# Batched 64x64 matmul on one core: b cast two tiles ahead into three bf16 buffers

## The chip, the cores and the metric

One core of one Trainium2 chip runs the kernel. The metric is the device time of one execution in microseconds (us). Before the change three runs gave 134.10, 134.24 and 134.47 us, median 134.24 us.

## The reference

`a` and `b` are float32 arrays of 1024 matrices of 64x64; the result is their product, matrix by matrix, in float32.

```python
def reference(a, b):
    return np.matmul(a, b).astype(np.float32)
```

The kernel rounds both operands to bf16 and accumulates in float32.

## The kernel before, in words

**Tiles.** The 1024 matrices are 16 tiles t of 64 matrices (`n_t` = 16), and two tiles make one step s of `a` (`n_s` = 8). A tile of b is 1 MB in float32, the result of a tile is 1 MB, a step of a is 2 MB.

**What becomes of b.** `load_b(t)` (L94 to L98) issues one DMA of a whole tile into a float32 buffer `b_sb`, of which there are three (`B_AHEAD = 3`); even tiles are issued on the queue of SyncE (SP), odd tiles on that of ScalarE (ACT). `cast(t)` (L169 to L181) turns `b_sb` into `b_bf`, a bf16 copy of which there are two buffers (pool `work`). Casts run on VectorE (DVE, L173) but for tile 0 (ACT, L173) and tile 15 (two quarters on ACT, L180, and two on DVE, L178). A load of tile t+3 may start when cast(t) has emptied its `b_sb`.

**What becomes of a.** `load_first_a` brings step 0 through SP and ACT into buffers of the result pool (L91). `load_a(s)` brings the others: three DMAs on the GpSimd (POOL) queue that cast to bf16 on the way (`a_sb`, L74), and one on SP that doesn't (`a_raw`, L78). There are three buffers of each. For the steps 0, 1, 6 and 7 `regroup` gathers the rows into `a_bf` (L106 for step 0; L109 and L112, on DVE, for the others), `transpose` turns pairs of columns on TensorE (PE, L138) and ACT copies the result to `at_sb` (L141). For the steps 2 to 5 (`ON_DVE`) `transpose_dve` does this on DVE (L128) with one cast of `a_raw` on ACT (L126). `spread(t)` then copies `at_sb` on DVE (L164, or L154 for the steps 2 to 5) into one of two block-diagonal tiles `at_bd`. It may overwrite it when the product of tile t-2 has been computed.

**The product.** `multiply(t)` issues 64 matmuls (L218) from `at_bd` and `b_bf` into two halves `o_ps` in PSUM, and eight copies (L206) from there to `o_sb`: on ACT, but for two of the eight on DVE in tiles 11 and 13, and half of them on DVE in tile 15. `store(t)` sends `o_sb` to the result one tile later (L195): on POOL up to tile 13, on SP and ACT for the last two.

**What sets the order.** The body is written out under a manual schedule: each engine runs its instructions in the order of the program text, and waits are for data and for free buffers. A DMA stands in the queue of the engine that issues it, in that engine's order. In iteration t of the main loop the order is this:

```python
if t + 1 < n_t:
    spread(t + 1)
    cast(t + 1)
if t + B_AHEAD < n_t:
    load_b(t + B_AHEAD)
...
multiply(t)
if t == 0:
    regroup(1)
    load_a(A_AHEAD)
    load_a(A_AHEAD + 1)
    transpose(1, 0)
    transpose(1, 1)
```

So on DVE cast(1) stands between spread(1) and regroup(1), and cast(2) behind spread(2). After `multiply` the other iterations have `transpose_dve`, `regroup` or `transpose` for step s+2. On SP the DMAs before the loop are those of `a` for step 0, b tile 0, `a_raw` of step 1, b tile 2 and `a_raw` of step 2; in the loop `a_raw` of steps 3 and 4 are issued in iteration 0, and b tile 4 behind them in iteration 1.

Of the kernel before, what the change touches and what calls it, by code (L numbers as in the profile page):

```python
# [9 lines left out]
bf16 = mybir.dt.bfloat16  # L10
# [3 lines left out]
def kernel(  # L14
# [19 lines left out]
    n_t, n_s = B // 64, B // 128  # L34
    A_AHEAD = 3
    B_AHEAD = 3
# [9 lines left out]
    a_pool = ctx.enter_context(tc.tile_pool(name="a_pool", bufs=A_AHEAD))  # L46
    b_pool = ctx.enter_context(tc.tile_pool(name="b_pool", bufs=B_AHEAD))
    work = ctx.enter_context(tc.tile_pool(name="work", bufs=2))
    o_pool = ctx.enter_context(tc.tile_pool(name="o_pool", bufs=8))
    t_psum = ctx.enter_context(  # L50
        tc.tile_pool(name="t_psum", bufs=4, space=bass.MemoryType.PSUM)
# [18 lines left out]
    def load_a(s):  # L70

        a_sb = a_pool.tile([128, 3, 16, 64], bf16, name="a_sb")
        for h in range(3):
            nc.gpsimd.dma_start(  # L74
                out=a_sb[:, h, :, :].rearrange("p v k -> p (v k)"), in_=a_v[s, h], single_packet=True
            )
        a_raw = a_pool.tile([128, 16, 64], fp32, name="a_raw")
        nc.sync.dma_start(out=a_raw[:].rearrange("p v k -> p (v k)"), in_=a_v[s, 3])  # L78
        a_tiles[s] = a_sb, a_raw

    def load_first_a():

        raw = [
            o_pool.tile([128, 8, 2, 2, 64], fp32, name="o_sb")[:].rearrange(
                "p gh j wl n -> p (gh j wl n)"
            )
            for _ in range(2)
        ]
        parts = [raw[h % 2][:, 1024 * (h // 2) : 1024 * (h // 2) + 1024] for h in range(4)]
        for h in range(4):  # L90
            (nc.scalar if h % 2 else nc.sync).dma_start(out=parts[h], in_=a_v[0, h])  # L91
        a_tiles[0] = parts

    def load_b(t):  # L94
        b_sb = b_pool.tile([128, 16, 128], fp32, name="b_sb")
        queue = nc.scalar if t % 2 else nc.sync
        queue.dma_start(out=b_sb[:], in_=b_v[t])  # L97
        b_tiles[t] = b_sb  # L98

    def regroup(s):  # L100
        a_sb = a_tiles.pop(s)
        a_bf = work.tile([128, 16, 4, 64], bf16, name="a_bf")
        if s == 0:
            for h in range(4):
                copy = nc.scalar.copy if h % 2 else nc.vector.tensor_copy
                copy(a_bf[:, :, h, :], a_sb[h].rearrange("p (v k) -> p v k", v=16))  # L106
        else:
            cast_sb, raw = a_sb
            nc.vector.tensor_copy(  # L109
                a_bf[:, :, 0:3, :], cast_sb[:].rearrange("p h v k -> p v h k")  # L110
            )
            nc.vector.tensor_copy(a_bf[:, :, 3, :], raw[:])  # L112
        abf_tiles[s] = a_bf
        at_tiles[s] = work.tile([128, 32, 4, 4, 4], fp32, name="at_sb")

    def transpose_dve(s, half):
        cast_sb, raw = a_tiles[s]
        if half == 0:
            at_tiles[s] = work.tile([128, 4, 8, 4, 4, 4], fp32, name="at_sb")
        for h in (2 * half, 2 * half + 1):  # L120
            rows = cast_sb[:, h, :, :] if h < 3 else None
            if h == 3:
                rows = work.tile([128, 16, 4, 64], bf16, name="a_bf")[:, 0:4, :, :].rearrange(
                    "p x y k -> p (x y) k"
                )
                nc.scalar.copy(rows, raw[:])  # L126
            pairs = rows.rearrange("p v k -> p (v k)").bitcast(fp32)
            nc.vector.transpose(  # L128
                at_tiles[s][:, h].rearrange("p g w mp vo -> p w vo g mp"),
                pairs.rearrange("p (vo w kp) -> p w vo kp", vo=4, w=4),  # L130
            )

    def transpose(s, j):
        a_cols = abf_tiles[s][:].rearrange("p v h k -> p v (h k)").bitcast(fp32)
        for wl in range(2):
            at_ps = t_psum.tile([128, 4, 128], fp32, name="at_ps")
            for vo in range(4):
                nc.tensor.transpose(  # L138
                    at_ps[:, vo, :], a_cols[:, 4 * vo + 2 * j + wl, :], identity[:]
                )  # L140
            nc.scalar.copy(  # L141
                at_tiles[s][:, :, 2 * j + wl, :, :],
                at_ps[:].rearrange("p vo (g mp) -> p g mp vo", mp=4),
            )

    def spread(t):
        bd = bd_tiles[t % N_BD]
        at_sb = at_tiles[t // 2]
        for h in range(4):
            rows = slice(32 * h, 32 * h + 32)  # L150
            if t // 2 in ON_DVE:
                for i in range(2):
                    block = 32 * (2 * (t % 2) + i)
                    nc.vector.tensor_copy(  # L154
                        bd[rows, 8 * i : 8 * i + 8, :, h, :, :].rearrange(
                            "p g w mp vo -> p (g w) (mp vo)"
                        ),
                        at_sb[block : block + 32, h].rearrange(
                            "p g w mp vo -> p (g w) (mp vo)"
                        ),  # L160
                    )
            else:
                half = slice(16 * (t % 2), 16 * (t % 2) + 16)
                nc.vector.tensor_copy(  # L164
                    bd[rows, :, :, h, :, :].rearrange("p g w mp vo -> p (g w) (mp vo)"),
                    at_sb[rows, half].rearrange("p g w mp vo -> p (g w) (mp vo)"),
                )

    def cast(t):  # L169
        b_bf = work.tile([128, 16, 128], bf16, name="b_bf")  # L170
        b_sb = b_tiles.pop(t)
        if t < n_t - 1:
            (nc.vector.tensor_copy if t else nc.scalar.copy)(b_bf[:], b_sb[:])  # L173
        else:
            for gq in range(4):
                rows = slice(4 * gq, 4 * gq + 4)
                if gq % 2:
                    nc.vector.tensor_copy(b_bf[:, rows, :], b_sb[:, rows, :])  # L178
                else:
                    nc.scalar.copy(b_bf[:, rows, :], b_sb[:, rows, :])  # L180
        bbf_tiles[t] = b_bf  # L181

    def store(t):
        for piece in held.pop(t):
            piece()
# [53 lines left out]
    with tc.manual_schedule():  # L239
        load_first_a()  # L240

        nc.vector.memset(warm[:, 0:1], 0.0)
        nc.scalar.copy(warm[:, 1:2], warm[:, 0:1])
        load_b(0)
        load_b(1)
        nc.vector.memset(bd_tiles[0][:], 0.0)  # L246
        make_identity(nc, identity)
        nc.gpsimd.memset(bd_tiles[1][:, 0:8], 0.0)
        load_a(1)
        load_b(2)  # L250
        nc.gpsimd.memset(bd_tiles[1][:, 8:16], 0.0)
        load_a(2)
        regroup(0)
        transpose(0, 0)
        transpose(0, 1)
        spread(0)
        cast(0)
        for t in range(n_t):
            s, half = t // 2, t % 2
            if t + 1 < n_t:  # L260
                spread(t + 1)
                cast(t + 1)
            if t + B_AHEAD < n_t:
                load_b(t + B_AHEAD)
            if half == 0 and 0 < s < n_s - 1 - A_AHEAD:
                load_a(s + 1 + A_AHEAD)
            if half == 0 and 0 < s < n_s - 1 and s + 1 not in ON_DVE:
                transpose(s + 1, 1)
# [7 lines that stand above are left out]
            if t and s + 2 in ON_DVE and (half or s):  # L276
                for part in [0, 1] if t == 1 else [half]:
                    transpose_dve(s + 2, part)
                if half:
                    a_tiles.pop(s + 2)  # L280
            elif half == 0 and 0 < s and s + 2 < n_s:
                regroup(s + 2)
            elif half == 1 and s + 2 < n_s:
                transpose(s + 2, 0)
            if t >= HOLD - 1:
                store(t - HOLD + 1)
        for t in range(n_t - HOLD + 1, n_t):
            store(t)
# [30 lines left out]
```

## Time and profile before

| | value |
|---|---|
| median of three runs | 134.24 us |
| the profiled execution | 134.24 us, of which the span of its instructions is 132.1 us |
| mean granted clock of TensorE | 0.693 |
| DVE busy | 100.7 us, 76% |
| ACT busy | 89.2 us, 68% |
| PE busy | 63.2 us, 48% |
| POOL busy | 32.0 us, 24% |
| read from HBM, written | 33.55 MB, 16.78 MB |
| cast of b on DVE (L173), mean of one | 1227 ns |
| four copies of `spread` on DVE (L164), mean of one | 724 ns |
| eight copies of `spread` on DVE (L154), mean of one | 436 ns |

How to read it: times in the text are microseconds from the start of the span. "2.1 us around the span" is the difference between the execution's time and its span. A timeline row gives the start, the time from the first instruction's start to the last one's end, the engine, the line, and in brackets how long the engine sat idle ahead of it and what ended that. DMA rows give the issuing queue (SPq, ACTq, POOLq) and the time from issue to landing. Digits in the row of an engine are its busy share in tenths, for each of 40 equal slices of 3.3 us.

### The profile page before, as it was taken

The page shows a single profiled execution, that of the slowest core. Times are in us where ns is not written, and L with a number is a line of the kernel's source. Part 1 is how long each engine was busy: PE and PEld are TensorE (multiplying, and loading weights), DVE is VectorE, ACT ScalarE, POOL GpSimd, SP SyncE. Part 2 cuts the span into 40 slices and gives each one's busy share as a digit, 9 for nine tenths or more (in the row PEclk, how much of TensorE's full clock was granted, in tenths as well). Part 3 has the DMA queues.
Part 4 walks back from the last instruction along what each step waited for, and adds up shares of the span by engine and source line. Part 5 has one row for each costly group of instructions (what it writes and reads, how often), then busy time and mean ns, then how long its engine had stood idle before and what let it go on. Part 6 is the DMA issues. An engine that isn't in the chain of part 4 may idle for free.

```text
span 132.1 us, 2719 instructions
## 1 busy us (share of the span) xinstructions
PE 63.2 (48%) x1088; PEld 60.5 (46%) x1088; DVE 100.7 (76%) x150; ACT 89.2 (68%) x159; POOL 32.0 (24%) x43
## 2 busy tenths in 40 slices
PE   0006406990733701909190737359709834677700
PEld 0006306980733701909190737259709734676700
DVE  5930399209999915999989998999999998598730
ACT  2225524999893790583989197929999996728970
POOL 8991000420074000702061302040203040312000
PEclk9999999999686555555555555555995995555555
DMA  3999999999999999999999999999999999999996
GB/s 83 351 336 310 309 313 277 288 301 327 326 305 385 371 308 298 395 385 396 327 282 357 402 395 347 296 326 387 399 392 394 394 392 387 398 399 396 364 324 201
DMA packets 19020, 44.99 MB, mean 341 GB/s; under 512 B 1088, under 2 KB 3136, under 8 KB 19008
## 3 DMA queue, kind: packets, MB, share of 16 engines
q0 software_dynamic: 6832, 20.19, 50.6%
q1 hardware_dynamic: 7120, 14.68, 30.8%
q10 hardware_dynamic: 5056, 9.96, 20.0%
q8 instruction: 8, 0.13, 0.4%
q14 instruction: 4, 0.03, 0.1%
HBM read 33.55 MB, written 16.78 MB: 381 GB/s over the span
## 4 chain that ended last, share of the span: by engine, by line
DMA 37%; DVE 27%; ACT 13%; PE 9%; issue 8%; ACTq 2%; SPq 1%
DMA b_sb<-in_b_dram 31%; DVE at_bd L154 11%; ACT o_sb L206 11%; DMA o_sb<-in_a_dram 6%; DVE b_bf L173 6%; PE o_ps L218 5%; DVE at_bd L164 4%; PE at_ps L138 3%; DVE at_sb L128 3%; DVE a_bf L109 1%; DVE a_bf L112 1%; ACTq L97 1%; ACT a_bf L126 1%; ACT a_bf L106 1%; ACT at_sb L141 1%
## 5 line engine op out<-in xcount | busy, mean ns | idle before, releaser
L206 ACT COPY o_sb<-o_ps 64x512 f32<-64x512 f32 x116 | 67.4, 581 | 19.2 <-PE o_ps L218 16.1
L218 PEld LDWEIGHTS <-at_bd 128*128 128x128 bf16 x1024 | 50.5, 125 | 52.9 <-DVE b_bf L173 44.7
L218 PE MATMUL o_ps<-b_bf,at_bd 128*128 128x64 bf16 x960 | 49.1, 231 | 49.4 <-DVE b_bf L173 42.7
L164 DVE COPY at_bd<-at_sb 32x1024 f32<-32x1024 f32 x32 | 23.2, 724 | 12.7 <-ACT at_sb L141 11.9
L154 DVE COPY at_bd<-at_sb 32x512 f32<-32x512 f32 x64 | 27.9, 436 | 1.3
L195 POOL DMA_DIRECT2D out_dram<-o_sb x14 | 15.5, 1108 | 47.5 <-ACT o_sb L206 30.7
L74 POOL DMA_DIRECT2D a_sb<-in_a_dram x21 | 12.4, 606 | 39.8 <-DVE at_sb L128 26.4
L173 DVE CAST b_bf<-b_sb 128x2048 bf16<-128x2048 f32 x14 | 17.2, 1227 | 6.4 <-DMA b_sb<-in_b_dram 6.0
L138 PE MATMUL at_ps<-identity,a_bf 128*128 128x128 f32 x64 | 11.2, 349 | 11.2 <-ACT a_bf L106 11.2
L138 PEld LDWEIGHTS at_ps<-identity,a_bf 128*128 128x128 f32 x64 | 10.3, 188 | 11.1 <-issue 11.1
L128 DVE STREAM_TRANSPOSE at_sb<-a_sb 128x512 f32<-128x512 f32 x12 | 12.0, 1062 | 0.0
L141 ACT COPY at_sb<-at_ps 128x512 f32<-128x512 f32 x16 | 8.5, 594 | 2.1 <-PE at_ps L138 2.0
L106 ACT CAST a_bf<-o_sb 128x1024 bf16<-128x1024 f32 x2 | 2.1, 1044 | 5.2 <-DMA o_sb<-in_a_dram 5.2
L128 DVE STREAM_TRANSPOSE at_sb<-a_bf 128x512 f32<-128x512 f32 x4 | 4.2, 1053 | 0.7 <-ACT a_bf L126 0.7
L126 ACT CAST a_bf<-a_raw 128x1024 bf16<-128x1024 f32 x4 | 4.2, 1046 | 0.7 <-DMA a_raw<-in_a_dram 0.6
L173 ACT CAST b_bf<-b_sb 128x2048 bf16<-128x2048 f32 x1 | 1.9, 1898 | 3.7 <-DMA b_sb<-in_b_dram 3.7
L206 DVE COPY o_sb<-at_ps 64x256 f32<-64x256 f32 x8 | 3.4, 422 | 1.3 <-PE at_ps L218 1.2
L246 DVE MEMSET at_bd<- 128x4096 f32 x1 | 3.5, 3472 | 0.8 <-issue 0.8
L218 PE MATMUL at_ps<-b_bf,at_bd 128*128 128x64 bf16 x64 | 3.6, 242 | 1.0 <-DVE at_bd L164 1.0
L106 DVE CAST a_bf<-o_sb 128x1024 bf16<-128x1024 f32 x2 | 2.8, 1385 | 1.7 <-DMA o_sb<-in_a_dram 1.7
L206 ACT COPY o_sb<-at_ps 64x256 f32<-64x256 f32 x8 | 2.9, 367 | 0.1
L180 ACT CAST b_bf<-b_sb 128x512 bf16<-128x512 f32 x2 | 1.1, 616 | 2.8 <-DMA b_sb<-in_b_dram 2.8
(16 smaller groups left out, 15.4 us busy)
## 6 DMA issues: line engine op xcount, KB each, us to landing
out_dram<-o_sb POOLq DMA_DIRECT2D x14, 1024.0 KB, 21.1
a_sb<-in_a_dram POOLq DMA_DIRECT2D x21, 256.0 KB, 16.0
a_raw<-in_a_dram SPq DMA_DIRECT2D x7, 512.0 KB, 16.9
o_sb<-in_a_dram SPq DMA_DIRECT2D x2, 512.0 KB, 5.8
o_sb<-in_a_dram ACTq DMA_DIRECT2D x2, 512.0 KB, 7.1
out_dram<-o_sb SPq DMA_DIRECT2D x2, 512.0 KB, 3.6
out_dram<-o_sb SPq DMA_DIRECT2D x2, 256.0 KB, 3.6
out_dram<-o_sb ACTq DMA_DIRECT2D x2, 256.0 KB, 3.1
```

Of the source, the lines that this page charges most:

```text
L74: nc.gpsimd.dma_start(out=a_sb[:, h, :, :].rearrange("p v k -> p (v k)"), in_=a_v[s, h], single_packet=True)
L106: copy(a_bf[:, :, h, :], a_sb[h].rearrange("p (v k) -> p v k", v=16))
L126: nc.scalar.copy(rows, raw[:])
L128: nc.vector.transpose(at_tiles[s][:, h].rearrange("p g w mp vo -> p w vo g mp"), pairs.rearrange("p (vo w kp) -> p w vo kp", vo=4, w=4),)
L138: nc.tensor.transpose(at_ps[:, vo, :], a_cols[:, 4 * vo + 2 * j + wl, :], identity[:])
L141: nc.scalar.copy(at_tiles[s][:, :, 2 * j + wl, :, :], at_ps[:].rearrange("p vo (g mp) -> p g mp vo", mp=4),)
L154: nc.vector.tensor_copy(bd[rows, 8 * i : 8 * i + 8, :, h, :, :].rearrange("p g w mp vo -> p (g w) (mp vo)"), at_sb[block : block + 32, h]. ...
L164: nc.vector.tensor_copy(bd[rows, :, :, h, :, :].rearrange("p g w mp vo -> p (g w) (mp vo)"), at_sb[rows, half].rearrange("p g w mp vo -> p ...
L173: (nc.vector.tensor_copy if t else nc.scalar.copy)(b_bf[:], b_sb[:])
L195: store_queue(t, lo).dma_start(out=o_v[t, :, lo : lo + n, :], in_=o_sb[:, lo : lo + n].rearrange("p gh j wl n -> p (gh j wl n)"),)
L206: copies[2 * par + wl](dst, src)
L218: nc.tensor.matmul(o_ps[:, gl, g % 2, j, :], at_bd[:, j, g, :, u], b_bf[:, g, 64 * u : 64 * u + 64], start=(u == 0), stop=(u == 1),)
```

## The change

`b_bf` moves out of the pool `work` (two buffers) into a pool of its own with three. Before the loop `cast(1)` is added behind `cast(0)`, with `load_b(3)` between them. In iteration t the cast is that of tile t+2 in place of t+1, and the load that of tile t+4 in place of t+3. Nothing else changes; the number of casts and loads is the same.

```diff
+    bf_pool = ctx.enter_context(tc.tile_pool(name="bf_pool", bufs=3))
...
     def cast(t):
-        b_bf = work.tile([128, 16, 128], bf16, name="b_bf")
+        b_bf = bf_pool.tile([128, 16, 128], bf16, name="b_bf")
...
         spread(0)
         cast(0)
+        load_b(B_AHEAD)
+        cast(1)
         for t in range(n_t):
             s, half = t // 2, t % 2
             if t + 1 < n_t:
                 spread(t + 1)
-                cast(t + 1)
-            if t + B_AHEAD < n_t:
-                load_b(t + B_AHEAD)
+            if t + 2 < n_t:
+                cast(t + 2)
+            if t + B_AHEAD + 1 < n_t:
+                load_b(t + B_AHEAD + 1)
```

In the changed order DVE runs spread(0), cast(1), spread(1), cast(2), regroup(1), spread(2), cast(3) and so on; SP issues b tile 4 between `a_raw` of step 2 and `a_raw` of step 3; ACT issues b tile 5 behind the copies L141 of step 1; and ACT's two quarters of cast(15) stand ahead of its copies of tile 13's result.

## The prediction

> **What bounds the kernel now.** The profiled execution took 134.24 us: its span of 132.1 us and 2.1 us around it. The median is the same 134.24 us, so sums on the span carry over. Read first the busy digits of VectorE and the DMA engines.
>
> ```profile
> DVE  5930399209999915999989998999999998598730
> DMA  3999999999999999999999999999999999999996
> ```
>
> DMA engines are busy from the second slice to the last but one. DVE is thin in slices 3 to 9 and again in 14, then full from 16 to 33. In the table by stretches DVE works 45.66 us of the 48 us from 61 to 109, and the rest is the 0.03 us between its 76 instructions; so a delay that DVE carries into this stretch isn't made up in it. The list of waits says what DVE and ACT lacked elsewhere.
>
> ```profile
> DVE at_bd L164 <- ACT at_sb L141: 11.9, 2, 6.0
> DVE b_bf L173 <- DMA b_sb<-in_b_dram: 6.0, 3, 4.2
> ACT b_bf L180 <- DMA b_sb<-in_b_dram: 2.8, 1, 2.8
> ```
>
> The columns are us in total, times, longest. The 11.9 us are startup (spread(0) and spread(2) wait for transposed a). The 6.0 are casts waiting for b: 4.2 at tile 4, then 0.41 and 1.37 at tiles 13 and 14. The 2.8 are tile 15 on ACT, and from there the chain of waits runs to the end. The change moves all of these. DVE's timeline of the startup:
>
> ```profile
> 17.61 3.50 DVE L164 COPY at_bd<-at_sb 32x1024 f32<-32x1024 f32 x5
> 21.15 1.23 DVE L173 CAST b_bf<-b_sb 128x2048 bf16<-128x2048 f32 x1
> 22.29 0.95 DVE L109 COPY a_bf<-a_sb 128x3072 bf16<-128x3072 bf16 x1
> 23.16 0.69 DVE L112 CAST a_bf<-a_raw 128x1024 bf16<-128x1024 f32 x1
> 29.84 2.83 DVE L164 COPY at_bd<-at_sb 32x1024 f32<-32x1024 f32 x4 [6.00 <-ACT at_sb L141]
> 32.71 1.23 DVE L173 CAST b_bf<-b_sb 128x2048 bf16<-128x2048 f32 x1
> ```
>
> Cast(1) comes at 21.15, regroup(1) ends at 23.85, its transposes and their copies bring spread(2) to 29.84, and cast(2) follows at 32.71. The deciding number is when b tile 2 lands. A window of the DMA view around its issue at 9.89 has only that load of b:
>
> ```profile
> b_sb<-in_b_dram SPq DMA_DIRECT2D x1, 0.5 KB, 21.8
> ```
>
> So it lands at 31.65, 1.1 us ahead of its cast in the old order. In the new order cast(2) stands ahead of regroup(1), whose data are there at 22.
>
> **Part 1, the start (loss).** spread(0) ends at 18.3. Cast(1) is next and waits for b tile 1: issued at 2.76, 17.4 us to landing, so 20.1; with 1.23 it ends at 21.4. spread(1) took 2.8 (18.33 to 21.12) and ends at 24.2. Multiply(0) isn't touched, it waits for ACT's cast(0) until 21.0. Then cast(2) waits from 24.2 to 31.65 and ends at 32.9. Behind it on DVE stand regroup(1) and all else; behind regroup(1) stand PE's 16 transposes, ahead of multiply(1) in PE's order, ACT's four copies with the issue of b tile 5, on POOL the loads of a for step 4 and store(0), on SP `a_raw` of step 4. Regroup(1) took 1.5 us from the cast's end (22.38 to 23.85): 34.4. The transposes took 3.2 (24.48 to 27.66), the last copy 0.6: 38.2. So spread(2) starts at 38.2 in place of 29.84, 8.4 late, with one cast more behind it (1.2): DVE is 7.2 us behind in work. DMA engines lose little: at 24 the tiles 2, 3 and 4 of b and some a are in the queues.
>
> **Part 2, tile 4 (gain).** The old SP order put b tile 4 behind two `a_raw` loads, the second of which waited for regroup(1).
>
> ```profile
> 51.18 1.23 DVE L173 CAST b_bf<-b_sb 128x2048 bf16<-128x2048 f32 x1 [4.24 <-DMA b_sb<-in_b_dram]
> 52.32 1.07 DVE L128 STREAM_TRANSPOSE at_sb<-a_sb 128x512 f32<-128x512 f32 x1
> ```
>
> This row also shows how a waiting cast holds DVE: the transpose behind it reads an `a_sb` of step 3, issued by 11.31 and landed, by the DMA rows, at most 21.7 us later, and still starts after the cast. In the new order tile 4 is issued at about 22, when cast(1) has freed its buffer and SP's stalled `a_raw` is out (10.64 plus 11.44). Even at the slowest landing of any b load (26.3 us) it is there at 48.4. Cast(4) comes at 38.2 plus spread(2) 2.8, cast(3) 1.2, four transposes 4.0 and spread(3) 3.0, so 49.2. The 4.2 us vanish: 7.2 - 4.2 = 3.0 us behind. Next could be tile 5: its issue on ACT moves from 35.18 to 38.2, behind the copies; at the median of 16.4 us it lands at 54.6, and cast(5) wants it at 49.2 + 1.2 + 1.9 (two transposes) + 3.4 (spread(4)) = 55.7. A margin of 1.1 us; I take no wait.
>
> **Part 3, the full stretch.** Work is the same. Two waits of DVE for ACT's cast of `a_raw` (0.40 and 0.35) go, as a cast now stands ahead of those transposes: 2.2 us behind at the end of it. The eight copies of L154 took 3.43 to 3.99 us a tile, 1.7 us over the minimum in the sum of eight tiles; the long ones lie beside POOL's issues, whose places shift: between -1 and +1, taken as 0. The third `b_bf` buffer adds no wait: cast(t+2) overwrites what multiply(t-1) read, and spread(t+1), just ahead, waits for that product already.
>
> **Part 4, the end.** Issues of b follow the casts. Cast(11) would end at 97.3 (before 99.04), so tile 14 lands at 97.3 + 16.1 = 113.4, wanted at 112.7 after spread(13): a wait of 0.7 for 1.37; tile 13's 0.41 goes. That saves 1.1. Ahead of spread(15) DVE now also has its half of cast(15), 0.8. So spread(15), which ended at 121.1, is 3.0 - 0.75 - 1.1 + 0.8 = 2.0 us late, and multiply(15) with it. On ACT the order turns against itself: cast(15) now stands ahead of tile 13's copies. Tile 15, issued about 102.5, lands at 116.9 to 118.9 (14.4 to 16.4 us), while tile 13's products are ready at about 115. Behind it ACT has 1.1 (cast), 3.6, 4.7 and 3.4 us of copies: 129.7 to 131.7, where it ended at 128.65. So this path is 1.1 to 3.1 late, DVE's 2.0. I take 1.9: **134.24 + 1.9 = 136.1 us**, with 135.2 to 137.4 for this case.
>
> The Trainium skill speaks for the change here: "DMA: Bandwidth & Descriptors", section "Anatomy of one DMA — SWDGE (gpsimd) path", fits a DMA at 2.0 us plus its bytes over 436e3 per us. That is 4.4 us for 1 MB (an estimate from that page, whose fit is for the other queue kind); tile 2 would be there at 14.3, cast(2) would wait for nothing, and 7.2 us of part 1 would fall away. The 21.8 us of this trace are five times that, so the fit isn't used.
>
> **Rivals.**
> *Faster: tile 2 lands in time.* The price of part 1 goes down by 1 us for each us that tile 2 lands earlier, down to 24.2. In the new order less of a is asked for while tile 2 is on its way, and the first loads of b landed in 16.6 and 17.4 us. Break even is at 31.65 - 1.9 = 29.7, a landing of 19.8 us; at 24.2 the wait is gone, and what is left is the gain of parts 2 to 4, limited by the DMA engines: their share is 0.87 in the 12.1 us from 120 on against some 1.06 before, (1.06 - 0.87) / 1.06 x 12.1 = 2.2 us that could be closed, so 132.0 us. Against it: all that competes with tile 2 was issued by 11.3, ahead of any change, and SP's queue ahead of it is the same.
> *Slower still: no payback.* Tile 5 takes as long as tile 2 did (21.8 in place of 16.4): cast(5) waits 4.3 us, 140.4. Half of that gives 138.3.
> *Even.* Tiles 14 and 15 land earlier than I say, as stores come later and compete less, POOL's shift gives 1 us back, and ACT isn't blocked by cast(15): 134.24 + 2.0 - 0.7 - 1.0 = 134.5.
> *The change doesn't deepen the loads.* There are still three `b_sb`, and tile t+4 takes the buffer that cast(t+1), not cast(t+2), freed. On ACT the issue stands behind the copies of tile t-1. Then loads come no earlier against their casts and only the order of DVE changes: tiles 13 to 15 wait as before, 1.1 more, 137.2; this lies in my case's range.
>
> **Numbers.** A measurement of this kernel tells about 0.3% (0.4 us) from no change. Forecast with the fourth rival 0.62, no payback 0.13, even 0.12, faster 0.13. The range takes in the even case and half of the missing payback: 134.0 to 138.5. Faster 0.13, same 0.12, slower 0.75.
>
> **What would show it.** Part 1: DVE idle some 7 us ahead of the second cast with b's DMA as its end, L109 at about 33, spread(2) near 38. Part 2: no wait at cast(4). Part 3: DVE full from 38 to about 112. Part 4: ACT waiting for b at L181 ahead of tile 13's copies. I am wrong if cast(2) starts before 29, or if DVE has idle time between 55 and 110 in which a delay is made up.

## The result and the profile after

The changed kernel takes **139.34 us** (five runs, 138.96 to 139.44) against 134.11 us of the kernel before beside it: ratio 1.037, 95% interval 1.035 to 1.039. It is slower by 5.2 us where 1.9 had been forecast. The profiled execution has a span of 137.6 us, 5.5 more than before.

Busy digits of VectorE and of the DMA engines, from the page of the changed kernel (a slice is now 3.44 us):

```profile
DVE  5930349107099999999999999999999999348540
DMA  3999999999999999999999999999999999973993
```

Count the slices from 0. In slices 7 to 10 DVE now has 1, 0, 7, 0 where it had 2, 0, 9, 9; the old hole of 1 and 5 in slices 14 and 15 is gone, and the full stretch runs from 11 to 33. Behind it DVE drops to 3 and 4, and the DMA engines, full there before, drop to 7 and 3 a slice later. So the loss is in two places, at the start and at the end, and the list of waits (us in total, times, longest) names both:

```profile
DVE at_bd L165 <- ACT at_sb L142: 10.3, 2, 5.9
DVE b_bf L174 <- DMA b_sb<-in_b_dram: 8.3, 3, 6.1
DVE o_sb L207 <- ACT o_sb L207: 4.0, 1, 4.0
ACT b_bf L181 <- DMA b_sb<-in_b_dram: 3.8, 1, 3.8
```

The 6.1 is cast(2). The wait of DVE's copies of a result for ACT's copies, 4.0 us once, isn't in the old list at all. (Lines are one higher than before, as the diff adds one.)

**The start**, DVE's timeline of the changed kernel:

```profile
20.71 1.23 DVE L174 CAST b_bf<-b_sb 128x2048 bf16<-128x2048 f32 x1 [2.04 <-DMA b_sb<-in_b_dram]
21.85 2.77 DVE L165 COPY at_bd<-at_sb 32x1024 f32<-32x1024 f32 x4
30.74 1.23 DVE L174 CAST b_bf<-b_sb 128x2048 bf16<-128x2048 f32 x1 [6.11 <-DMA b_sb<-in_b_dram]
31.88 0.95 DVE L110 COPY a_bf<-a_sb 128x3072 bf16<-128x3072 bf16 x1
32.75 0.68 DVE L113 CAST a_bf<-a_raw 128x1024 bf16<-128x1024 f32 x1
37.88 2.83 DVE L165 COPY at_bd<-at_sb 32x1024 f32<-32x1024 f32 x4 [4.45 <-ACT at_sb L142]
...
48.78 1.23 DVE L174 CAST b_bf<-b_sb 128x2048 bf16<-128x2048 f32 x1
```

Cast(2) holds DVE for 6.1 us, regroup(1) (L110) comes at 31.9 in place of 22.3, spread(2) at 37.9 in place of 29.8. Cast(4) at 48.8 waits for nothing. So far this is the forecast, step by step.

**The end**, DVE and then ACT in the timeline of the changed kernel:

```profile
114.25 3.25 DVE L165 COPY at_bd<-at_sb 32x1024 f32<-32x1024 f32 x4
117.53 0.76 DVE L179 CAST b_bf<-b_sb 128x512 bf16<-128x512 f32 x2
122.25 1.39 DVE L207 COPY o_sb<-o_ps 64x512 f32<-64x512 f32 x2 [3.95 <-ACT o_sb L207]
123.67 3.09 DVE L165 COPY at_bd<-at_sb 32x1024 f32<-32x1024 f32 x4
128.74 3.48 DVE L207 COPY o_sb<-at_ps 64x256 f32<-64x256 f32 x8 [1.98 <-PE at_ps L219]
```

```profile
108.92 4.75 ACT L207 COPY o_sb<-o_ps 64x512 f32<-64x512 f32 x8
117.52 1.14 ACT L181 CAST b_bf<-b_sb 128x512 bf16<-128x512 f32 x2 [3.85 <-DMA b_sb<-in_b_dram]
118.67 3.55 ACT L207 COPY o_sb<-o_ps 64x512 f32<-64x512 f32 x6
123.02 2.35 ACT L207 COPY o_sb<-o_ps 64x512 f32<-64x512 f32 x4 [0.80 <-ACT o_sb L207]
```

Read them together. ACT has copied tile 12 at 113.7 and waits 3.85 us for b tile 15. Only then does it copy tile 13, to 122.2. DVE, which has two copies of the same half of tile 13 to make, starts them at 122.25, the moment ACT ends, and spread(15) and multiply(15) stand behind them. The chain of the changed kernel that ended last has exactly these links, each starting within 0.05 us of the one ahead of it:

```profile
121.64 0.59 ACT o_sb L207
122.23 0.02 issue
122.25 0.68 DVE o_sb L207
...
123.67 0.69 DVE at_bd L165
...
126.82 1.90 PE at_ps L219 x32
```

The waits written into the program have this link too, in both kernels: DVE's first copy of tile 13 waits for a result buffer's store, for PE, and for ACT, and the ACT value it waits for is that of ACT's last copy of the same half.

In the old profile the link can't be seen. ACT's and then DVE's timeline of the kernel before:

```profile
112.96 3.55 ACT L206 COPY o_sb<-o_ps 64x512 f32<-64x512 f32 x6 [1.68 <-issue]
119.29 1.14 ACT L180 CAST b_bf<-b_sb 128x512 bf16<-128x512 f32 x2 [2.77 <-DMA b_sb<-in_b_dram]
```

```profile
115.31 1.23 DVE L173 CAST b_bf<-b_sb 128x2048 bf16<-128x2048 f32 x1 [1.37 <-DMA b_sb<-in_b_dram]
116.57 1.39 DVE L206 COPY o_sb<-o_ps 64x512 f32<-64x512 f32 x2
117.99 3.09 DVE L164 COPY at_bd<-at_sb 32x1024 f32<-32x1024 f32 x4
```

DVE's copies began at 116.57, behind ACT's (112.96 plus 3.55, so 116.51) and also behind DVE's own cast(14) (115.31 plus 1.23, so 116.54).

### The profile page after: what moved, and what is told of

It is laid out like the page before. It is cut to its first block, busy times and chain, and to the rows that moved or that the text cites. A ratio compares the mean times of both kernels' runs of the same rounds, so it can differ in the third digit from the quotient of the medians.

```text
span 137.6 us, 2713 instructions
## 1 busy us (share of the span) xinstructions
PE 64.2 (47%) x1088; PEld 61.0 (44%) x1088; DVE 101.3 (74%) x150; ACT 89.6 (65%) x159; POOL 32.1 (23%) x43
## 3 DMA queue, kind: packets, MB, share of 16 engines
q0 software_dynamic: 6832, 20.19, 48.8%
## 5 line engine op out<-in xcount | busy, mean ns | idle before, releaser
L219 PE MATMUL o_ps<-b_bf,at_bd 128*128 128x64 bf16 x960 | 49.1, 231 | 44.9 <-DVE at_bd L155 22.3
L174 DVE CAST b_bf<-b_sb 128x2048 bf16<-128x2048 f32 x14 | 17.7, 1263 | 8.7 <-DMA b_sb<-in_b_dram 8.3
L139 PE MATMUL at_ps<-identity,a_bf 128*128 128x128 f32 x64 | 11.9, 364 | 20.2 <-ACT a_bf L107 11.5
L207 DVE COPY o_sb<-o_ps 64x512 f32<-64x512 f32 x4 | 2.8, 689 | 4.0 <-ACT o_sb L207 4.0
L98 ACT MOVE_SHAPE b_sb<-in_b_dram x8 | 0.5, 64 | 7.2 <-DVE b_bf L174 7.1
```

The lines of the kernel that those rows point to most:

```text
L139: nc.tensor.transpose(at_ps[:, vo, :], a_cols[:, 4 * vo + 2 * j + wl, :], identity[:])
L207: copies[2 * par + wl](dst, src)
L219: nc.tensor.matmul(o_ps[:, gl, g % 2, j, :], at_bd[:, j, g, :, u], b_bf[:, g, 64 * u : 64 * u + 64], start=(u == 0), stop=(u == 1),)
```

## The experiments

After the result the theory was: two separate losses, a smaller one at the start (cast(2) ahead of regroup(1)) and a larger one at the end (cast(15) ahead of tile 13's copies on ACT, and through them on DVE). The rivals were that the start's delay is all of it, or that deeper loads cost the DMA engines. The first four kernels take the places apart. Each ratio is to the kernel before beside it, whose median was 134.19 to 134.44 us; where a time is set against the changed kernel's 139.34 us, that goes across comparisons and is good to some 0.3 us.

**Cast(15) back behind spread(15)**, the rest as changed.

```diff
-            if t + 2 < n_t:
+            if t + 2 < n_t - 1:
                 cast(t + 2)
+            if t == n_t - 2:
+                cast(t + 1)
```

> The changed kernel, but with cast(15) in its old place behind spread(15). Main theory (two separate losses: cast(2) holds DVE at the start, some 2.4 us carried to the end, and cast(15) holds ACT's copies of tile 13 and through them DVE's copies of tile 13, spread(15) and multiply(15), 3.95 us): the second loss goes, 135.3 to 136.3 us. Rival A (the delay of the start is all of it and the end would be late in any order): 138.8 to 139.5. Rival B (deeper loads of b cost the DMA engines, casts don't matter): 138.8 to 139.5.

135.16 us (ratio 1.0056, 1.0033 to 1.0080): 4.2 of the 5.2 us are gone, a little more than expected. ACT now copies tile 13 at 114.00 and casts at 117.46 without a wait, and spread(15) starts at 119.01, 1.0 late in place of 5.7. Both rivals fall. From ACT's and DVE's timelines of this run:

```profile
114.00 3.56 ACT L207 COPY o_sb<-o_ps 64x512 f32<-64x512 f32 x6 [0.30 <-ACT o_sb L207]
117.46 1.14 ACT L181 CAST b_bf<-b_sb 128x512 bf16<-128x512 f32 x2
...
117.59 1.39 DVE L207 COPY o_sb<-o_ps 64x512 f32<-64x512 f32 x2 [0.39 <-ACT o_sb L207]
119.01 3.09 DVE L165 COPY at_bd<-at_sb 32x1024 f32<-32x1024 f32 x4
```

**Cast(2) behind regroup(1)**, cast(15) as changed.

```diff
-            if t + 2 < n_t:
+            if 0 < t < n_t - 2:
                 cast(t + 2)
...
                 regroup(1)
+                cast(2)
```

> The changed kernel, but with cast(2) behind regroup(1) in place of ahead of it; cast(15) stays ahead of tile 13's copies. Main theory: spread(2) starts near 32 in place of 37.9, DVE is 4 to 5.5 us earlier through the full stretch, the loss at the end stays: 134.0 to 135.5 us. Rival A (start is everything): 133 to 134. Rival B (DMA engines): 138.5 to 139.5.

137.86 us (1.0244, 1.0222 to 1.0265): 1.5 us better than the changed kernel, where 4 to 5 had been expected: a miss. The start counts, but for less than the theory said.

**Both moves together.**

> The changed kernel with both of these moves: cast(2) behind regroup(1), cast(15) behind spread(15). Main theory: both losses go and the early load of tile 4 stays as a gain, limited by the 2.2 us that the DMA engines idle at the end: 131.5 to 133.0 us, faster than both kernels. Rival A: the same as the run with only cast(2) moved. Rival B: 138 to 139.5.

134.23 us (0.9982, 0.9965 to 0.9998), a miss: the two losses are gone, and that leaves the old time, with no gain to show. The two moves nearly add up (4.2 and 1.5 us alone, 5.1 together): 135.16 less 134.23 is 0.9 us for the start once the end is mended. Why the start is worth so little stands in DVE's timeline of this run:

```profile
31.57 1.23 DVE L174 CAST b_bf<-b_sb 128x2048 bf16<-128x2048 f32 x1 [6.27 <-DMA b_sb<-in_b_dram]
...
37.52 1.23 DVE L174 CAST b_bf<-b_sb 128x2048 bf16<-128x2048 f32 x1 [1.98 <-DMA b_sb<-in_b_dram]
...
61.18 1.23 DVE L174 CAST b_bf<-b_sb 128x2048 bf16<-128x2048 f32 x1 [2.10 <-DMA b_sb<-in_b_dram]
```

Regroup(1) is early again (23.74), and DVE waits at casts 2, 3 and 6 for b instead. With cast(2) ahead of regroup(1) and the end mended, in the first run, cast(6) came at 62.23 without a wait: of the 8 us that regroup(1) gains, 1.05 are left at cast(6), and 0.9 reach the end. In this stretch an order that removes one wait of DVE for b brings up the next.

**The kernel before, with only the load of tile 4 early.** This is the gain of Part 2, the forecast's largest, by itself.

```diff
-            if t + B_AHEAD < n_t:
+            if t != 1 and t + B_AHEAD < n_t:
                 load_b(t + B_AHEAD)
+            if t == 0:
+                load_b(B_AHEAD + 1)
```

> The kernel before, with one edit: the load of b tile 4 is issued in iteration 0, ahead of the loads of a for steps 3 and 4, in place of iteration 1 behind them. Casts and buffers are the old ones. Main theory (this is all that the change has to gain): cast(4) doesn't wait, DVE is 4 us ahead through the full stretch, the end is limited by the last loads of b and the DMA engines: 131.5 to 133.0 us. Rival (a gain at tile 4 is given back at the end, where the casts wait for tiles 13 to 15): 133.8 to 134.5.

133.95 us (0.9952, 0.9937 to 0.9967). The rival's number is right: 4.1 us are gained at cast(4) and only 0.5 arrive. The place isn't the one it named: DVE's timeline of this run shows that most of it goes at tile 6.

```profile
47.08 1.23 DVE L173 CAST b_bf<-b_sb 128x2048 bf16<-128x2048 f32 x1
...
54.73 1.23 DVE L173 CAST b_bf<-b_sb 128x2048 bf16<-128x2048 f32 x1
...
64.26 1.23 DVE L173 CAST b_bf<-b_sb 128x2048 bf16<-128x2048 f32 x1 [3.15 <-DMA b_sb<-in_b_dram]
```

Casts 4 and 5 are 4.1 and 3.6 us earlier than before; cast(6), which came at 64.72, comes at 64.26.

The next three kernels ask what in the place of cast(15) costs.

**All of cast(15) on DVE, at the same early place.**

```diff
-                if gq % 2:
+                if gq >= 0:
                     nc.vector.tensor_copy(b_bf[:, rows, :], b_sb[:, rows, :])
```

> The changed kernel, with all four quarters of cast(15) on DVE, at the same early place. Main theory (the loss at the end is ACT's wait for b tile 15 ahead of tile 13's copies, which DVE's copies of tile 13, spread(15) and multiply(14) wait for): ACT isn't held, DVE waits for the landing instead, to about 117.5, and spread(15) starts near 120.5 in place of 123.7: 135.8 to 137.0 us. Rival (cast(15) is too early on whatever engine): 138.5 to 139.5.

135.66 us (1.0104, 1.0071 to 1.0136): 3.7 us better, just past what was expected, though the cast is as early as ever. ACT isn't held, and DVE's copies of tile 13 start at 118.36, with no wait.

**Cast(15) without its wait.**

```diff
-        b_sb = b_tiles.pop(t)
+        b_sb = b_tiles[14 if t == n_t - 1 else t]
```

> The changed kernel, but cast(15) reads the float32 buffer of tile 14, which has landed some 4 us before; the load of tile 15 is still made, its data are not used, so tile 15 of the result is computed from tile 14's b. Order and work of all engines are those of the changed kernel. Main theory (it is the wait for the landing, not the place or the 1.1 us of work): ACT's wait of 3.85 us goes, 135.0 to 136.2 us. Rival (the order on ACT costs by itself): 138 to 139.5.

135.90 us (1.0101, 1.0044 to 1.0158): 3.4 us better, with the changed kernel's order and work. So it is the wait for the landing; the place in ACT's order and the 1.1 us of casting are left with some 0.7 us, by which this run is slower than the one with cast(15) back, and the intervals of the two overlap.

**All copies of tile 13 on ACT**, which cuts the link to DVE.

```diff
-                if half and t % 2 and t > 2 * max(ON_DVE):
+                if half and t == n_t - 5:
```

> The changed kernel, with all eight copies of tile 13 on ACT (two of them were on DVE). This cuts the link from ACT's copies to DVE: spread(15) no longer waits for cast(15), but ACT has 1.2 us more to copy and multiply(14) still waits for ACT's copies to free its PSUM. Main theory: spread(15) starts near 118.5, the end is then ACT's own chain, 1.5 to 2.5 us better: 136.8 to 138.0 us. Rival (the link is not what counts, ACT's chain alone sets the end): 139.3 to 140.5.

137.83 us (1.0259, 1.0212 to 1.0307): 1.5 us better, inside what was expected. The wait on ACT is still there (3.77 us), but spread(15) starts at 117.61, and DVE then idles 6.04 us for PE, whose product of tile 14 waits for ACT's copies of tile 13 to empty its PSUM (the trace names spread(15) as the end of that wait, which ended at the same time, 120.44, but writes a tile that this product doesn't read):

```profile
116.93 1.14 ACT L181 CAST b_bf<-b_sb 128x512 bf16<-128x512 f32 x2 [3.77 <-DMA b_sb<-in_b_dram]
118.08 9.49 ACT L207 COPY o_sb<-o_ps 64x512 f32<-64x512 f32 x16
```

So cutting the link to DVE is worth 1.5 us net of 1.2 us more work on ACT; what is left of the loss at the end is then ACT's own chain.

The last four ask where a gain goes.

**Tile 4 early, and b ahead of a in SP's queue.**

```diff
-        a_raw = a_pool.tile([128, 16, 64], fp32, name="a_raw")
-        nc.sync.dma_start(out=a_raw[:].rearrange("p v k -> p (v k)"), in_=a_v[s, 3])
-        a_tiles[s] = a_sb, a_raw
+        a_tiles[s] = a_sb, None
+        if s <= 4:
+            load_raw(s)
...
+    def load_raw(s):
+        a_raw = a_pool.tile([128, 16, 64], fp32, name="a_raw")
+        nc.sync.dma_start(out=a_raw[:].rearrange("p v k -> p (v k)"), in_=a_v[s, 3])
+        a_tiles[s] = a_tiles[s][0], a_raw
...
+            if t in (3, 5, 7):
+                load_raw((t + 7) // 2)
```

> The kernel before with b tile 4 early (as in the earlier run), and with the SP loads of a for the steps 5, 6 and 7 issued behind those of b tiles 6, 8 and 10 in place of ahead of them. Theory (the 4.2 us that tile 4 gains are given back at tile 6, as its load stands behind that of a in SP's queue: a 3.15 us wait of cast(6) in the earlier run): tile 6 lands 2 to 4 us earlier, that wait all but goes, 132.8 to 133.8 us, limited by the DMA engines at the end. Rival (DMA engines are full, what isn't waited for at tile 6 is waited for at 13 to 15): 133.8 to 134.3.

134.38 us (1.0005, 0.9982 to 1.0028). The step was right and the sum was wrong: cast(6) now comes at 61.07 without a wait, and DVE stays 3 to 4 us ahead of the old kernel to the end, yet the time is the old one, beyond what either theory or rival gave. Nor is it the rival's waits: those at casts 13 and 14 are 0.81 and 1.09 us here, 0.41 and 1.37 before. The DMA view around the last store, first of this kernel (issued at 124.43), then of the kernel before (issued at 128.27):

```profile
out_dram<-o_sb ACTq DMA_DIRECT2D x1, 256.0 KB, 6.1
```

```profile
out_dram<-o_sb ACTq DMA_DIRECT2D x1, 256.0 KB, 2.9
```

It is issued 3.8 us earlier and takes 3.2 us longer: it lands at 130.5 against 131.2. From 116 to 130 the DMA engines' share is 1.01 in this kernel and 1.00 before. By their busy share they are full whichever engine is early, so the earlier issue only queues longer. Full is not the same as fast: in the slices that the old page shows as 9 the engines moved between 277 and 402 GB/s. Whether other transfers would bring the end forward, no run here tells.

**Three `b_bf` buffers alone**, in the old order.

```diff
+    bf_pool = ctx.enter_context(tc.tile_pool(name="bf_pool", bufs=3))
...
-        b_bf = work.tile([128, 16, 128], bf16, name="b_bf")
+        b_bf = bf_pool.tile([128, 16, 128], bf16, name="b_bf")
```

> The kernel before, with three b_bf buffers in a pool of their own and nothing else changed: casts and loads in the old order. Theory: nothing waits for a b_bf buffer, within 0.3% of before, 133.8 to 134.6 us. Rival (the new pool moves buffers in SBUF, and something else pays for it): off by more than 0.4 us.

133.86 us (0.9973, 0.9956 to 0.9991): inside the expectation. The buffer costs nothing; where the 0.3% under the kernel before come from, no run here tells.

**Two tiles ahead from tile 3 on, with neither loss**, beside **tile 4 early alone, again**.

```diff
-            if t + 2 < n_t:
+            if t in (1, n_t - 2):
+                cast(t + 1)
+            if 0 < t < n_t - 3:
                 cast(t + 2)
```

> The changed kernel without its two losses: cast(2) in its old place behind spread(2), cast(3) right behind it, from there on two tiles ahead, and cast(15) behind spread(15). Theory (casting ahead brings nothing by itself; the gain is the early load of tile 4, most of which is given back at tile 6 and at the end, where the DMA engines are full): the same as the kernel before with only tile 4 early, 133.6 to 134.3 us. Rival (the deeper cast is worth its 2 us of waits once nothing blocks): 131.8 to 133.2 us.

> The kernel before with only tile 4's load early once more, beside the run with casts ahead from tile 3, on the same chip and in more rounds: 133.6 to 134.1 us, 0.2% to 0.6% under before.

134.01 us (0.9979, 0.9962 to 0.9995) with the casts ahead, and 134.04 us (0.9986, 0.9971 to 1.0000) with the old casts, whose 0.14% is less than the 0.2% to 0.6% expected. The two are the same: casting b two tiles ahead brings nothing in itself here. The early load of tile 4 gave 0.9952 in one comparison and 0.9986 in the other, so it gains at most half a per cent, and no kernel here beats the old one by more.

## Why the prediction was wrong

The sign and the start were right; the size was wrong (139.3 us for 136.1, with 138.5 as the upper bound), and one step of Part 4 is the main cause.

- **Part 1, the start.** Right in every link. b tile 2 landed 20.5 us from its issue at 10.18, so 30.7 where 31.65 was taken; spread(2) started at 37.9 where 38.2 was worked out.
- **Part 2, tile 4.** Right. The load was issued at 22.9 and landed in 15.0 us, at 37.9; cast(4) came at 48.8 without a wait (49.2 worked out), and tile 5 was in time. At spread(5) DVE is 58.34 - 54.29 = 4.05 us late with one cast of 1.23 more behind it, 2.8 behind in work; the text has 3.0.
- **Part 3, the full stretch.** Right: the two waits for ACT's cast of `a_raw` are gone (they are 0.75 of the 2.34 us that the opening paragraph put down to gaps between instructions), and spread(13) ends at 112.9 where 112.7 was worked out. The shift by POOL's issues came out near 0.
- **Part 4, the end.** Tile 14 (wait of 0.19 for 0.7) and the landing of tile 15 (117.5; 116.9 to 118.9 worked out) are right, and so is ACT's wait ahead of tile 13's copies: ACT ended at 131.1, inside 129.7 to 131.7 (the text's 128.65 for the old end counts the last store's issue; the copies ended at 128.24). The step that failed is "So this path is 1.1 to 3.1 late, DVE's 2.0. I take 1.9": it treats ACT and DVE as two paths beside each other. DVE's two copies of tile 13 wait for ACT's copies of that half, so ACT's wait runs into DVE: spread(15) began 5.7 us late (123.67 against 117.99), and DVE's last copies ended 5.7 us late. Of the 5.7 us, 3.95 are the wait for ACT that the sum put at nothing; without it spread(15) would have been 1.7 late, where 2.0 was worked out. The old order hid the link behind cast(14); the waits in the program had it. The three runs that take the wait off ACT (135.2, 135.7 and 135.9 us) give back 3.4 to 4.2 us, and the one that cuts only the link 1.5.
- **The size of the start.** It was about right. The sum's 2.0 us hold 0.8 for cast(15) ahead of spread(15); with cast(15) back behind it the sum leaves 1.2, and that run had spread(15) 1.0 late, 135.16 us against 134.44 for the kernel before and 134.23 with both moves. The 2.4 us in the expectation of that run left out the waits for tiles 13 and 14 that go.
- **The rivals.** Tile 2 landed 0.9 us earlier than taken, far from 24.2. "No payback" didn't happen. "The change doesn't deepen the loads" doesn't hold for tiles 13 and 14, which were waited for less (0 and 0.19 us for 0.41 and 1.37); tile 15 landed at 117.5, where it had been 119.2. That a gain of DVE is worth its full size, on which the faster rival's 132.0 us rests in part, was refuted: 4.1 us at cast(4) were 0.2 to 0.6 us at the end.

On the page "DMA: Bandwidth & Descriptors" of the Trainium skill, section "Anatomy of one DMA — SWDGE (gpsimd) path", the fit, made on DMAs that GpSimd issues, would have 1 MB land in 4.4 us (an estimate from that page). In these runs b tile 4 took 15.0 us in the changed kernel and 22.4 us with cast(2) behind regroup(1), where POOL's loads of a were issued 7.7 us earlier (25.4 for 33.1). The measurement decides: with three queues in use the fit didn't tell when a load of this kernel lands.

## What to carry to other kernels

When an instruction that waits for a DMA is moved up in an engine's order, list everything that stands behind it there, and then everything on other engines that waits for that: two engines that empty the same PSUM tile can be one path, as here, even if the old profile shows no wait between them because the old order hid it. The waits written into the program tell. A gain at one engine is worth only what the next limit leaves: before adding it to the end, ask whether the DMA engines are full from there on. Here a deeper prefetch of data that arrive just in time moved the wait and didn't remove it.

## What the runs showed of the hardware that was not expected

- An earlier last store did not land earlier: it was issued at 124.4, 127.1 and 128.3 in three kernels (tile 4 early with b ahead of a; both moves; the old one), and by the DMA rows the latest landing of any store was at 130.9, 131.1 and 131.2. It isn't a fixed floor: with cast(15) back, whose POOL loads of a for step 4 started at 33.05 in place of 23.54, the last store was issued at 127.1 and landed at 132.2.
- The landing of one 1 MB load goes with what the other queues hold. b tile 4 was issued between 22.2 and 23.1 in eleven kernels. In the five where POOL's loads of a for step 4 started between 32.6 and 33.2 it took 14.8 to 15.1 us; in the six where they started between 23.0 and 25.4 it took 21.4 to 22.4 us. No run moved those loads alone, so the cause is likely, not shown.
- A cast on DVE that took 1.23 us elsewhere took 1.48 us twice in the changed kernel, at 62.36 and at 76.21; both lie beside a store's issue on POOL (61.75 to 62.81 and 75.56 to 76.66). Whether the one causes the other, no run tells.
